# Keys in place, wider loads and write-backs on VectorE in a row-maximum kernel

## The chip, the cores and the metric

The kernel runs on one core of one Trainium2 chip. A core has several engines that run their own instruction streams and meet at semaphores; here ACT (ScalarE), POOL (GpSimd) and DVE (VectorE) compute, and SP (SyncE) issues the transfers, which 16 DMA engines carry out. TensorE is not used. The metric is the device time of one execution in microseconds, lower is better. The kernel before takes 1251.36 us, the median of 3 runs from 1251.27 to 1251.43.

## The reference

```python
x = np.random.randn(32, 2048, 2048).astype(np.float32)
x[np.random.rand(32, 2048, 2048) < 0.1] = np.nan

def reference(x, axis):          # axis = -1
    return np.nanmax(x, axis=axis).astype(np.float32)
```

The input is 65,536 rows of 2048 float32 values, 537 MB; about one value in ten is NaN. The output is the maximum of each row that leaves NaN out, 65,536 values. Each input byte is needed once.

## The kernel before, in words

**The arithmetic.** VectorE's maximum has to be kept from seeing a NaN. The kernel looks at the upper 16 bits of each float as a signed integer h. A finite value has h up to 0x7F7F, the NaN of this input has 0x7FC0. ACT computes a *key* from h with a Prelu (in `act`, called at line 493): for h up to 0x7F7F the key is 0x7F7F - h, for the NaN it is 0x7F7F + 128, as an unsigned 16-bit integer. A *write-back* then puts 0x7F7F - key into the upper half of the float. That gives h again for an ordinary value, and the upper half of minus infinity for a NaN. After that VectorE takes plain float maxima (a `tensor_reduce`, line 419 in `maxima`). Rows that were all NaN end as minus infinity and are turned into NaN at the end of each part of the output (`find`, lines 296 to 327).

**The tiles.** A tile holds some number of quarter rows for each of the 128 partitions; a quarter row is 512 floats. `TILES` (lines 17 to 46) is a plan written out by hand, one entry for each tile with three lists, all in quarter rows: the sizes of its loads; its chunks, each a pair of the sizes of the keys and the sizes of the write-backs; and the sizes of its maxima. A plain number among the write-backs is done by POOL; a pair `(n, w)` with w of 0 or more is done by ACT, w keys later; `(n, -1)` is done by VectorE, a case that the code has and the plan before does not use. So `([28], [([7], [7]), ([9], [9]), ([12], [12])], [16, 12])` is one load of 28 quarter rows (7 MB in all), three keys of 7, 9 and 12, three write-backs of the same sizes on POOL, and two maxima, of 16 and of 12. There are 74 tiles: one of 4, 46 of the kind just shown, and 27 others of 28 whose loads are cut ever finer towards the end; from tile 47 on ACT does some write-backs.

**Buffers.** Three input buffers `xt` of 28 quarter rows (`WIDE = 7` rows) take turns. Keys go to three separate dense 16-bit buffers `kt` of 12 quarter rows each (`KEYS`, `NKEYS`), so ACT reads every second half-word of `xt` and writes a dense `kt`; the write-back reads `kt` and writes every second half-word of `xt`. Before ACT reuses a `kt` it waits for the write-backs from it (`freed`, lines 379 to 389; `EARLY` names tiles that wait for the next buffer too).

**The order.** Each engine runs its instructions in the order in which the loop from line 440 issues them; `Order.add` puts a semaphore wait only where one is needed. For each tile the loads are issued first, then for each key: the key on ACT, the write-backs that it completes (`write`, lines 347 to 377), and every maximum whose quarter rows are all written back (`maxima`). The loads of tile n+3 (line 464, all on SP's queue) wait for the last maximum of tile n. `PARTS` gives after which tile a finished part of the output is fixed up on POOL, or on VectorE for the last one. The stores of the results come last on SP, after the last load.

Of the kernel before, what the change touches and what calls it, by code (L numbers as in the profile page):

```python
# [9 lines left out]
D = 2048  # L10

Q = D // 4
# [6 lines left out]
    + [([28], [([7], [7]), ([9], [9]), ([12], [12])], [16, 12])] * 46  # L19
# [6 lines left out]
    + [([28], [([7], [7]), ([9], [9]), ([12], [12])], [16, 12])] * 2  # L26
# [23 lines left out]
    tuple(range(1, 17)),  # L50
    tuple(range(17, 33)),
    tuple(range(33, 49)),
    tuple(range(49, 65)),
    (0,) + tuple(range(65, 74)),
# [5 lines left out]
    (0, 1, 16, 18),  # L60
    (1, 17, 32, 34),
    (2, 33, 48, 52),
    (3, 49, 64, 67),
    (4, 0, 72, None),
    (4, 73, 73, "dve"),
)

WIDE = 7
BUFS = 3

KEYS = 3 * D
NKEYS = 3
# [3 lines left out]
HEADS = 1  # L76
# [3 lines left out]
EARLY = tuple(range(47)) + (47, 48, 49, 50, 51, 52, 53, 54, 55, 56, 57, 58, 59, 60, 61, 68,)  # L80
# [105 lines left out]
def kernel(  # L186
# [15 lines left out]
    nc = tc.nc  # L202
# [15 lines left out]
    for tiles in GROUPS:  # L218
# [9 lines left out]
    firsts = [  # L228
        nc.alloc_sbuf_tensor(f"xt{i}", [P, WIDE * D], i32).ap() for i in range(HEADS)
    ]  # L230
    sing = ctx.enter_context(tc.tile_pool(name="sing", bufs=1))
    top, warm = scalars[:, 0:1], scalars[:, 1:2]
    xts = firsts + [
        sing.tile([P, WIDE * D], i32, name=f"xt{i}") for i in range(HEADS, BUFS)
    ]
    kts = [sing.tile([P, KEYS], u16, name=f"kt{i}") for i in range(NKEYS)]
# [23 lines left out]
    for number in range(HEADS):  # L260
        (c,) = TILES[number][0]
        gi, base = place[number]
        to = xts[number][:, 0 : c * Q]
        head = nc.sync.dma_start(  # L264
            out=dataclasses.replace(to, dep_tracking_offset=to.offset + P * WIDE * D),
            in_=groups[gi][0][:, base : base + c * Q],
        )
        tc.no_tile_sem_insts.add(head.ins.name)
        heads.append(head)

    with tc.tile_critical() as section:  # L271
# [75 lines left out]
        def write(number, a, b, k, kp, e, i, back):  # L347
            to = xts[number % BUFS][:, a:b].bitcast(i16)[:, 1::2]
            pair = pairs[number].get(i)
            name = pair and f"pair{number}_{pair[0]}"  # L350
            if back == "act":
                e = act(
                    [e], name, out=to, in_=kp, func=ACT.Copy, bias=float(TOP), scale=-1.0
                )
            else:
                kw = dict(
                    out=to,
                    in0=kp,
                    scalar1=-1.0,
                    scalar2=float(TOP),  # L360
                    op0=ALU.mult,
                    op1=ALU.add,
                )
                if back == "dve":
                    e = dve([e], nc.vector.tensor_scalar, **kw)
                else:
                    e = pool([e], name, **kw)
            state["clock"] += 1
            both = [(a, b, k, back, (state["clock"], order.count[back] + (back != "dve")))]
            if pair:  # L370
                if name not in half:
                    half[name] = both
                    return
                both += half.pop(name)
            for a, b, k, back, when in both:
                kfree[k][back] = max(kfree[k].get(back, ((0, 0), None)), (when, e))
                clean[number].append((a, b, e, back))
# [13 lines left out]
        def maxima(last):  # L391

            while state["tile"] <= last:
# [16 lines left out]
                xt = xts[number % BUFS]  # L410
# [29 lines left out]
        for number, (loads, chunks, reds) in enumerate(TILES):  # L440
# [3 lines left out]
            for ks, bs in chunks:  # L444
                assert sum(ks) * Q <= KEYS
# [12 lines left out]
            xt, before = xts[number % BUFS], free[number % BUFS]  # L458
            assert number < BUFS or state["tile"] > number - BUFS
            landed = []  # L460
# [21 lines left out]
            for step, c in enumerate(keys):  # L482
# [3 lines left out]
                if used + fresh.get(step, 0) > KEYS:  # L486
                    key = (key + 1) % NKEYS
                    used = 0
                    assert all(h[3] != key for h in held)
                    assert all(q[2] != key for v in half.values() for q in v)  # L490
                    kold = freed(key, (key + 1) % NKEYS) if number in EARLY and at + c == end else freed(key)
                    kfree[key] = {}
                e_key = act(
                    kold + here,
                    out=kts[key][:, used : used + c],
# [6 lines left out]
                used += c  # L502
# [104 lines left out]
```

## Time and profile before

| what | value |
|---|---|
| median of the runs | 1251.36 us |
| the profiled execution's own time | 1251.48 us |
| its span, first to last instruction | 1249.6 us |
| DVE busy | 1109.5 us (89%), 183 instructions |
| ACT busy | 980.1 us (78%), 286 |
| POOL busy | 1159.9 us (93%), 256 |
| data moved | 537.19 MB, mean 430 GB/s |
| the input queue's packets | 99.5% of the span of 16 DMA engines |

Busy is time in which an engine executes; the three engines work side by side, so the shares do not add. The rows of the profile name an engine, a line of the kernel, an operation, and what it writes and reads, output ahead of the arrow. All of ACT's work stands at line 277, POOL's write-backs at line 287 and VectorE's maxima at line 294, because helpers record them; `kt<-xt` on ACT is a key, `xt<-kt` a write-back, `acc<-xt` a maximum. Idle time is put down to what ended it.

### The profile page before, as it was taken

Reading aid. Unit: us, or ns where it says so; the run is one execution under the profiler, and the core shown is the slowest. Engines: PE = TensorE matmul, PEld = TensorE weight load, DVE = VectorE, ACT = ScalarE, POOL = GpSimd, SP = SyncE. Lnnn points to the kernel's source line nnn. Section 1 sums busy time; section 2 is a strip of 40 time slices with the busy share of each in tenths; the row PEclk is TensorE's granted clock in tenths of the full one; section 3 lists DMA queues with packets and bytes.
Section 4 is the critical chain, followed back from the end, with each engine's and each line's share of the span. In section 5 each row is a group of like instructions: output and inputs, shape, how many; then the busy total and the mean of one; then the engine's idle time right before and its main releaser. Section 6 shows DMA issues by size and latency. Waiting matters only on the chain.

```text
span 1249.6 us, 916 instructions
## 1 busy us (share of the span) xinstructions
DVE 1109.5 (89%) x183; ACT 980.1 (78%) x286; POOL 1159.9 (93%) x256
## 2 busy tenths in 40 slices
DVE  0888889888889888889888888988898999999999
ACT  3777777777777777777777777799877799999998
POOL 2999999999999999999999999967999987999988
DMA  9999999999999999999999999999999999999997
GB/s 415 441 411 441 441 441 430 423 441 441 437 415 441 441 439 426 428 441 439 437 419 439 441 439 430 424 441 439 437 422 436 439 437 433 422 436 428 429 429 316
DMA packets 16806, 537.19 MB, mean 430 GB/s; under 512 B 2592, under 2 KB 2592, under 8 KB 5152
## 3 DMA queue, kind: packets, MB, share of 16 engines
q1 hardware_dynamic: 16800, 537.14, 99.5%
q14 instruction: 6, 0.05, 0.0%
HBM read 536.87 MB, written 0.26 MB: 430 GB/s over the span
## 4 chain that ended last, share of the span: by engine, by line
POOL 37%; DVE 29%; DMA 25%; ACT 8%; issue 1%; SPq 0%
POOL xt L287 37%; DVE acc L294 29%; DMA xt<-in_x_dram 25%; ACT kt L277 7%; ACT xt L277 2%; POOL late L309 0%; POOL acc L323 0%; SPq L264 0%; SPq L469 0%; DVE acc L301 0%; SPq L602 0%; SPq L271 0%
## 5 line engine op out<-in xcount | busy, mean ns | idle before, releaser
L287 POOL TENSOR_SCALAR xt<-kt 128x3584 int16<-128x3584 uint16 (+10 forms) x241 | 1154.8, 4792 | 83.7 <-ACT kt L277 67.9
L294 DVE TENSOR_REDUCE acc<-xt 128x4 f32<-128x8192 f32 (+4 forms) x182 | 1109.3, 6149 | 137.8 <-POOL xt L287 130.9
L277 ACT ACTIVATE kt<-xt 128x3584 uint16<-128x3584 int16 (+10 forms) x252 | 913.9, 3663 | 262.5 <-DMA xt<-in_x_dram 222.6
L277 ACT ACTIVATE xt<-kt 128x512 int16<-128x512 uint16 (+7 forms) x32 | 68.6, 2145 | 0.7
L309 POOL TENSOR_SCALAR late<-acc 128x112 int32<-128x112 f32 (+1 forms) x5 | 2.8, 559 | 0.4
L323 POOL TENSOR_TENSOR acc<-acc,late 128x112 int32<-128x112 int32 (+1 forms) x5 | 2.0, 399 | 0.4
L277 ACT ACT_TABLE_LOAD x1 | 1.3, 1283 | 1.3 <-SPq L271 1.3
L329 POOL MEMSET scalars<- 128x1 f32 x1 | 0.1, 99 | 0.9 <-SPq L271 0.9
L588 POOL MEMSET const-float32-0.0<- 128x1 f32 x1 | 0.1, 99 | 0.2 <-issue 0.2
L277 ACT ACTIVATE scalars<-scalars 128x1 f32<-128x1 f32 x1 | 0.2, 203 | 0.0
L301 DVE SCALAR_TENSOR_TENSOR acc<-acc 128x7 f32<-128x7 f32 x1 | 0.2, 167 | 0.0
L588 POOL MEMSET const-bfloat16-1.0<- 128x1 bf16 x1 | 0.1, 102 | 0.0
L588 POOL MEMSET const-uint8-127<- 128x1 uint8 x1 | 0.1, 102 | 0.0
L588 POOL MEMSET const-float32-1.0<- 128x1 f32 x1 | 0.1, 99 | 0.0
## 6 DMA issues: line engine op xcount, KB each, us to landing
xt<-in_x_dram SPq DMA_DIRECT2D x62, 7168.0 KB, 22.5
xt<-in_x_dram SPq DMA_DIRECT2D x2, 4096.0 KB, 19.4
xt<-in_x_dram SPq DMA_DIRECT2D x2, 3584.0 KB, 25.6
xt<-in_x_dram SPq DMA_DIRECT2D x5, 1280.0 KB, 29.4
xt<-in_x_dram SPq DMA_DIRECT2D x4, 1536.0 KB, 24.2
xt<-in_x_dram SPq DMA_DIRECT2D x2, 3072.0 KB, 26.3
xt<-in_x_dram SPq DMA_DIRECT2D x1, 5632.0 KB, 19.5
xt<-in_x_dram SPq DMA_DIRECT2D x2, 2816.0 KB, 24.8
```

The costliest lines, as they stand in the source:

```text
L277: lambda: nc.scalar.activation(**kw),
L287: lambda: nc.gpsimd.tensor_scalar(**kw),
L294: return order.add("dve", nc.vector, lambda: do(**kw), deps)
L301: lambda: engine.scalar_tensor_tensor(out=acc, in0=acc, scalar=0.0, in1=acc, op0=ALU.mult, op1=ALU.add),
L309: lambda: engine.tensor_scalar(out=none, in0=acc, scalar1=LEAST, scalar2=float(0x00400000), op0=ALU.is_lt, op1=ALU.mult,),
L323: lambda: engine.tensor_tensor(out=bits, in0=bits, in1=none, op=ALU.add),
L329: e_top = order.add("pool", nc.gpsimd, lambda: nc.gpsimd.memset(top, EDGE), [])
L588: nc = _bacc.Bacc("TRN2", target_bir_lowering=False, num_devices=1)
```

## The change

- In tiles 0 to 37 (`PLAIN = 38`) the key is written over the upper half of its own float in `xt`, and the write-back reads it there. No `kt` is used and ACT has no wait for one.
- The three input buffers become parts of one tensor of 3 x 32 quarter rows. Tiles 0 to 35 (`FULL = 36`) use buffers of 32 quarter rows, later tiles buffers of 28 (`NARROW`); the space between these holds two of the three key buffers for the later tiles.
- 31 tiles have one load of 32 quarter rows; four more tiles of 32 have two loads. There are 69 tiles in place of 74.
- In tiles 1 to 37 and in a few later ones VectorE does one of the write-backs, 5 quarter rows in most, in the same form as POOL's (`tensor_scalar`).
- The sizes of the other tiles, the groups of rows, the parts of the output and the list `EARLY` follow from the new division.

```diff
-    + [([28], [([7], [7]), ([9], [9]), ([12], [12])], [16, 12])] * 46
...
+    + [([32], [([12], [(5, -1), 7]), ([12], [12]), ([8], [8])], [12, 12, 8])] * 31
+    + [([23, 9], [([18, 6], [(6, -1), 6, 12]), ([8], [8])], [12, 12, 8])]
+    + [([19, 13], [([12], [(5, -1), 7]), ([10], [10]), ([10], [3, 7])], [12, 12, 8])]
+    + [([12, 20], [([12], [(2, -1), 10]), ([12], [12]), ([8], [8])], [12, 12, 8])]
+    + [([15, 17], [([12, 8, 6, 6], [(2, -1), 10, 5, 7, 8])], [12, 12, 8])]
+    + [([28], [([9], [5, (4, -1)]), ([7], [7]), ([7], [7]), ([5], [5])], [4, 12, 12])]
+    + [([28], [([10], [(5, -1), 5]), ([6], [6]), ([9], [9]), ([3], [3])], [16, 12])]
...
+    + [([28], [([9], [9]), ([11], [11]), ([8], [(8, -1)])], [8, 20])]
...
+    + [([28], [([10], [10]), ([10], [10]), ([8], [(8, -1)])], [8, 20])]
...
-WIDE = 7
+WIDE = 8
+FULL = 36
+PLAIN = 38
+
+NARROW = (0, 17 * D // 2, 31 * D // 2)
...
+    full = nc.alloc_sbuf_tensor("xt", [P, BUFS * WIDE * D], i32).ap()
...
+    keys_ = full.bitcast(u16)
+    kts = [
+        sing.tile([P, KEYS], u16, name="kt"),
+        keys_[:, 14 * D : 14 * D + KEYS],
+        keys_[:, 45 * D : 45 * D + KEYS],
     ]
...
+    def room(number):
+        n = number % BUFS
+        if number < FULL:
+            return full[:, n * WIDE * D : (n + 1) * WIDE * D]
+        return full[:, NARROW[n] : NARROW[n] + 7 * D]
...
+            if number == PLAIN:
+                for k in (1, 2):
+                    kfree[k] = {"dve": ((0, 0), done_at[FULL - 1])}
...
-                if used + fresh.get(step, 0) > KEYS:
+                if number < PLAIN:
+                    key = 0
+                    kx = xt[:, at : at + c].bitcast(u16)[:, 1::2]
+                elif used + fresh.get(step, 0) > KEYS:
...
+                if number >= PLAIN:
+                    kx = kts[key][:, used : used + c]
+                    used += c
                 e_key = act(
                     kold + here,
-                    out=kts[key][:, used : used + c],
+                    out=kx,
                     in_=xt[:, at : at + c].bitcast(i16)[:, 1::2],
...
-                    kp = kts[key][:, used - (at - lo) : used - (at - lo) + n]
+                    kp = (
+                        kts[key][:, used - (at - lo) : used - (at - lo) + n]
+                        if number >= PLAIN
+                        else xt[:, lo : lo + n].bitcast(u16)[:, 1::2]
+                    )
```

More of the change, by code (lines that the diff above doesn't have):

```diff
@@ L78 @@
 LANES = 14
-EARLY = tuple(range(47)) + (47, 48, 49, 50, 51, 52, 53, 54, 55, 56, 57, 58, 59, 60, 61, 68,)
+EARLY = (0, 1, 2, 3, 4, 5, 6, 7, 8, 9, 10, 11, 12, 13, 14, 15, 16, 17, 18, 19, 20, 21, 22, 23, 24, 25, 26, 27, 28, 29, 30, 31, 32, 33, 34, 35, 36, 37, 38, 39, 40, 41, 42, 43, 44, 45, 46, 47, 48, 49, 50, 51, 52, 53, 54, 55, 56, 63)
 TOP = 0x7F7F
@@ L262 @@
         gi, base = place[number]
-        to = xts[number][:, 0 : c * Q]
+        to = room(number)[:, 0 : c * Q]
         head = nc.sync.dma_start(
-            out=dataclasses.replace(to, dep_tracking_offset=to.offset + P * WIDE * D),
+            out=dataclasses.replace(to, dep_tracking_offset=to.offset + P * BUFS * WIDE * D),
             in_=groups[gi][0][:, base : base + c * Q],
@@ L347, in write @@
         def write(number, a, b, k, kp, e, i, back):
-            to = xts[number % BUFS][:, a:b].bitcast(i16)[:, 1::2]
+            to = room(number)[:, a:b].bitcast(i16)[:, 1::2]
             pair = pairs[number].get(i)
@@ L375, in write @@
             for a, b, k, back, when in both:
-                kfree[k][back] = max(kfree[k].get(back, ((0, 0), None)), (when, e))
+                if number >= PLAIN:
+                    kfree[k][back] = max(kfree[k].get(back, ((0, 0), None)), (when, e))
                 clean[number].append((a, b, e, back))
@@ L409, in maxima @@
                 over.sort(key=lambda w: (w[3] == "act") == later)
-                xt = xts[number % BUFS]
+                xt = room(number)
                 lo = done - 1 if done % D else done
@@ L444 @@
             for ks, bs in chunks:
-                assert sum(ks) * Q <= KEYS
+                assert number < PLAIN or sum(ks) * Q <= KEYS
                 assert sum(ks) == sum(b[0] if isinstance(b, tuple) else b for b in bs)
@@ L457 @@
             xg = groups[gi][0]
-            xt, before = xts[number % BUFS], free[number % BUFS]
+            xt, before = room(number), free[number % BUFS]
             assert number < BUFS or state["tile"] > number - BUFS
+            if number == PLAIN:
+                for k in (1, 2):
+                    kfree[k] = {"dve": ((0, 0), done_at[FULL - 1])}
             landed = []
@@ L492 @@
                     kfree[key] = {}
+                if number >= PLAIN:
+                    kx = kts[key][:, used : used + c]
+                    used += c
                 e_key = act(
                     kold + here,
-                    out=kts[key][:, used : used + c],
+                    out=kx,
                     in_=xt[:, at : at + c].bitcast(i16)[:, 1::2],
```

31 lines of the change are left out of this document (12 added, 19 removed), and 44 rows, old and new, of the table TILES.

## The prediction

> Predicted: 1251.1 us, no change that a measurement can tell, because the 16 DMA engines already carry the input without a gap and the edit moves no byte less. What could spoil that is a new write-back on VectorE that has to fit into the period of one load.
>
> **What bounds the kernel now.** I read the busy shares by stage first, then the waits, then the chain that ended last, then the groups of one shape, then the end of the timeline. The five stages below are: first big load, one tile, tiles 2 to 61, the rest up to the store, and the end. Columns are length, busy time of each engine, clock, DMA share and GB/s.
>
> ```profile
> core 0: us, DVE busy (x) ACT busy (x) POOL busy (x), PEclk, DMA share, GB/s
> 0.00:22.49 22.49, 2.29 (x1) 3.40 (x3) 2.77 (x6) 1.00 0.98 414
> 22.49:39.43 16.94, 4.06 (x1) 12.45 (x4) 13.51 (x3) 1.00 1.00 433
> 39.43:1054.97 1015.54, 911.12 (x123) 779.72 (x191) 968.73 (x186) 1.00 1.00 434
> 1054.97:1242.53 187.56, 187.31 (x57) 182.40 (x87) 172.10 (x59) 1.00 1.00 427
> 1242.53:1249.60 7.07, 4.72 (x4) 2.12 (x3) 2.83 (x4) 1.00 0.14 37
> ```
>
> The DMA share is 1.00 from 22.49 to 1242.53 and the rate 434 GB/s in the long stage: transfers are never held up. The long stage is 60 loads of 28 quarter rows, 1015.54 / 60 = 16.93 us each, 0.6045 us a quarter row. POOL is busy 968.73 / 60 = 16.15 us of a period, VectorE 15.19, ACT 13.00. So POOL is near the period, but the transfers set it.
>
> ```profile
> ACT kt L277 <- DMA xt<-in_x_dram: 222.6, 63, 15.0
> DVE acc L294 <- POOL xt L287: 130.9, 59, 23.0
> ...
> ACT kt L277 <- POOL xt L287: 39.6, 59, 1.5
> ...
> SPq L469 <- DVE acc L294: 1151.7, 70, 37.8
> ```
>
> ACT waits for data, every engine behind it for the one ahead. SP's wait for VectorE is the ring of three buffers: the load of tile n+3 is issued after the last maximum of tile n. One turn of it, from the chain:
>
> ```profile
> 90.18 3.20 ACT kt L277
> 93.46 4.20 POOL xt L287
> 97.65 0.08 issue
> 97.73 5.35 POOL xt L287
> 103.11 15.16 DVE acc L294 x2
> 118.28 22.67 DMA xt<-in_x_dram
> ```
>
> The load is issued at 118.28 and lands 22.67 us later, though it takes 16.93: it stood behind the load ahead of it for 5.74 us. That is the room before the DMA engines could run dry. The end of the run:
>
> ```profile
> 0.74 0.37 SPq L264 DMA_DIRECT2D xt<-in_x_dram  x1
> ...
> 5.62 1.91 ACT L277 ACTIVATE kt<-xt 128x2048 uint16<-128x2048 int16 x1 [2.77 <-DMA xt<-in_x_dram]
> ...
> 1227.09 19.99 DVE L294 TENSOR_REDUCE acc<-xt 128x1 f32<-128x2048 f32 x9
> 1242.53 5.11 SPq L556 DMA_DIRECT2D out_dram<-acc  x3
> 1247.12 0.17 DVE L301 SCALAR_TENSOR_TENSOR acc<-acc 128x7 f32<-128x7 f32 x1
> ```
>
> The first store waits for the last load and leaves at 1242.53; VectorE ends at 1247.29, the span at 1249.6. The profiled execution took 1251.48 us, 1.88 outside its span, and stands 0.12 above the median of 1251.36.
>
> **The change part by part.** The prices, each the mean of its shape in ns, the figure ahead of a row's second bar:
>
> ```profile
> L294 DVE TENSOR_REDUCE acc<-xt 128x3 f32<-128x6144 f32 x61 | 399.2, 6545 | 1.1 <-POOL xt L287 1.1
> L287 POOL TENSOR_SCALAR xt<-kt 128x6144 int16<-128x6144 uint16 x51 | 359.2, 7042 | 4.5 <-ACT kt L277 0.6
> L277 ACT ACTIVATE kt<-xt 128x6144 uint16<-128x6144 int16 x60 | 319.3, 5322 | 35.7 <-POOL xt L287 35.5 <-DMA xt<-in_x_dram 0.2
> ...
> L287 POOL TENSOR_SCALAR xt<-kt 128x3584 int16<-128x3584 uint16 x57 | 239.2, 4197 | 23.9 <-ACT kt L277 20.5
> L277 ACT ACTIVATE kt<-xt 128x3584 uint16<-128x3584 int16 x59 | 188.1, 3189 | 199.0 <-DMA xt<-in_x_dram 198.2 <-POOL xt L287 0.7
> L294 DVE TENSOR_REDUCE acc<-xt 128x2 f32<-128x4096 f32 x27 | 118.4, 4412 | 0.2 <-POOL xt L287 0.2
> ...
> L287 POOL TENSOR_SCALAR xt<-kt 128x2560 int16<-128x2560 uint16 x8 | 24.4, 3055 | 2.0 <-ACT kt L277 1.6
> ...
> L277 ACT ACTIVATE xt<-kt 128x512 int16<-128x512 uint16 x10 | 7.7, 768 | 0.2
> ...
> L277 ACT ACTIVATE kt<-xt 128x512 uint16<-128x512 int16 x8 | 4.7, 613 | 0.0
> ...
> L277 ACT ACTIVATE xt<-kt 128x4096 int16<-128x4096 uint16 x1 | 4.8, 4767 | 0.0
> ```
>
> *Loads.* 31 loads of 32 quarter rows, 19.34 us each at the pace above, take the place of loads of 28; four more tiles of 32 come in two loads. Same bytes, 111 loads on SP before and after, no DMA added. Pieces of 64 KB a partition instead of 56 KB have no row: splitting or a slower long piece could cost, a longer piece could save. The pace is 434 GB/s with long pieces and 427 in the last stage with pieces down to 2 KB, so 8 KB more on an already long piece should be worth under 0.1%. I take 0, ends -1 and +2 us.
>
> *ACT.* In tiles 0 to 37 the key goes back into its own word, every second half-word, instead of into a dense buffer. A dense key costs (5322 - 3189) / 2560 = 0.833 ns an element. ACT's writes that land in every second half-word cost (4767 - 768) / 3584 = 1.116 ns, 0.197 us fixed. Nothing shows both sides strided over the same words. Ends: 0.833 (the reading alone was strided there already), and 1.40 if the same words on both sides cost that difference of 0.283 once more. I take 1.116, the row with the same output. Keys of 12, 12 and 8 quarter rows are then 7.05, 7.05 and 4.77, 18.9 us of 19.34. ACT would be the bound from (19.34 - 3 x 0.197) / 16384 = 1.144 ns. The waits for key buffers (39.6 us in all) go; ACT waits longer for data instead, so nothing is gained.
>
> *POOL.* It writes 27 of the 32 quarter rows, pieces of 7, 12 and 8: 4.20 + 7.04 + 4.77 (3584 and 512 more) + three issues of 0.08 = 16.25 us. It now also reads every second half-word; ACT read so at 0.833 ns. Ends: (7042 - 4197) / 2560 = 1.111 ns as before, and 1.39 with the same 0.283 added; taken 1.111. It binds from 1.335. Its four fix-ups for all-NaN rows go to other tiles; about 1.1 us each lies in POOL's idle 3 us.
>
> *VectorE.* Per tile it gains one write-back of 5 quarter rows, 2560 elements (W), and its maxima are 12, 12 and 8: 6.545 + 6.545 + 4.412, less two overlaps of 0.08 (15.16 in the chain for a pair whose means add to 15.23), 17.34. W has no row. VectorE's cheapest instruction, the 0.17 us one at 1247.12, is the low end; its rate of one element in (6545 - 4412) / 2048 = 1.042 ns with 0.145 fixed makes 2.81, and POOL's own 2560 takes 3.055, the high end. A maximum reads 4 bytes an element, W 2. By bytes W is a maximum of 1280 words, 1.48, which is also halfway between 0.17 and 2.81; I take 1.48. With 0.06 for the maximum's wait on W and 0.08 less where W follows, VectorE needs 18.8 us of 19.34 and fits up to W = 2.0.
>
> One tile, counted from its landing: keys end at 7.07, 14.12, 18.9. POOL writes 7 quarter rows from 7.14 to 11.34, 12 from 14.19 to 21.23, 8 to 26.1. In the first tile W follows POOL's 7; the maximum of 12 can start near 12.9, the second at 21.25 when POOL is done, and the third ends at 32.13. That is 12.8 us after the next landing (11.2 today: 118.28 less 90.18 and a period of 16.93), and the next W runs from 12.7 to 14.19. The load three on is issued 6.5 us before the engines run dry: no gap, and the pattern repeats. Behind SP's wait stand only later loads.
>
> *Tiles 36 to 68.* Tiles 36 and 37 need ACT 14336 x 1.116 + 4 x 0.197 = 16.8 of 16.93. The 8-quarter W of tiles 42 and 46 (0.145 + 4096 x 0.521 = 2.28) take VectorE to 17.3 against 16.93, 0.4 us of lag each; the room of over 5 us covers them and the next tiles, at 15.1, win back 1.8 each. The last eleven tiles, 308 quarter rows, have nearly the same maxima as before and cost VectorE about 167.5 us by these prices on either side.
>
> *The end.* The last landing stays near 1242.5. After it one quarter row still needs key 0.61, write-back 0.77, a whole-row maximum 2.28 (2048 x 1.042 + 0.145), the fix 0.17 and the store's 2.31 (1247.29 to 1249.6): 6.1, against 7.07 today. So the new end pieces can win at most 0.9; I take 0.3, between nothing and that.
>
> Sum: 1251.48 + 0 (loads) + 0 (ACT, POOL, VectorE, under the transfers) - 0.3 = 1251.2 as a profiled time; less 0.12, 1251.1.
>
> [...]
>
> **The rivals.**
>
> *VectorE and POOL shut each other out (slower).* For: W is due from 12.7 to 14.19 and POOL's long write at 14.19, and both work on the same words. Against: no wait in the trace shows maxima and POOL hindering each other, VectorE being busy 15.19 and POOL 16.15 of 16.93 us. If they exclude, the loop W + 7.04 + 0.02 + 10.88 - 0.08 = W + 17.86 has to stay under 19.34: it decides from W = 1.48, my own value. Above it the lag grows each tile; after 1.5 us W comes behind POOL's 12 and waits until 21.23. The tile then ends at 40.1, and three periods are 40.1 + 19.34 + 2.1 (issue to landing in an empty queue: 0.37 + 0.74 to 5.62, less 4 x 0.6045): 20.5 us each. Some 30 tiles x 1.15 = +34, 1285 us. [...]
>
> *VectorE becomes the bound (slower).* W at VectorE's known rate, 2.81: 20.1 against 19.34, 0.79 a tile. Room of 4.4 us (6.5 less 2.1) hides 6 tiles, 27 more pay: +21, 1272; at POOL's 3.055, 1279. For: one element in 1.042 ns is all that VectorE's rows show. Against: those read whole words.
>
> *Halves in place are dearer (slower).* ACT at 1.18 ns needs 19.9: 0.58 x 35 = +20, 1271; POOL at 1.39 needs 20.1, 1275. ACT at 1.40 would need 23.5, +147, 1398. For: no row reads and writes the same words strided. Against: reading strided costs ACT nothing above 0.833.
>
> *The end shortens and longer pieces speed the transfers (faster).* 0.9 and 1 us together, 1249.5; more has no row, so a gain over 0.2% (2.5 us, which is what I take a measurement of this kernel to tell from no change) is hardly to be had.
>
> **How the numbers follow.** Forecast 0.56 (own range 1249.9 to 1253.5, the load ends with the tail); shut out 0.15; VectorE the bound 0.12; halves dearer 0.10, of which the far end 0.02; a lag that the tiles of 28 don't win back, 2.5 to 6 us, 0.05; faster by more than 2.5 us 0.02. The range takes in the forecast, the lag, VectorE's bound and the near halves, 0.81: 1249.9 to 1279. Slower 0.15 + 0.12 + 0.10 + 0.05 = 0.42, same 0.56, faster 0.02.
>
> **What would show it.** Right: DMA share 1.00 and about 19.34 us between ACT's waits for data; ACT's in-place 6144 near 7.05 and POOL's at 7.04; VectorE's 2560 near 1.48 and starting about 12.7 us after a landing; the first store near 1242.5. Wrong: a gap in the DMA rate in the first three quarters; VectorE's 2560 at 2.8; waits of several us ahead of W with POOL busy, or POOL's writes drawn out beside W; ACT idle for data near zero.

## The result and the profile after

The changed kernel takes 1264.2 us (1261.87 to 1266.14, four runs), the kernel before 1251.39 beside it: a ratio of 1.0102 with a 95% interval of 1.0079 to 1.0125. It is slower by 12.8 us, where no change was forecast. The profiled execution took 1266.14 us, with a span of 1264.0.

The page of the changed kernel: the span, the busy times, and the rate in 40 slices of 31.6 us.

```profile
span 1264.0 us, 1010 instructions
DVE 1194.2 (94%) x251; ACT 1125.6 (89%) x275; POOL 1073.0 (85%) x248
GB/s 413 442 440 431 431 431 431 431 432 431 431 431 438 444 440 433 436 431 431 422 436 433 376 385 436 377 436 436 434 430 414 436 436 426 435 428 433 429 428 307
```

The first 22 slices stay around the full rate, a few per cent up and down. The worst slices, 376, 385 and 377, lie between 695 and 822 us. The busy time by stage, with columns as in the prediction: first wide load, one tile, tiles 2 to 31, the tiles in which the division changes, the rest up to the first store, and the end.

```profile
0.00:24.97 24.97, 2.29 (x1) 3.95 (x3) 2.76 (x6) 1.00 1.00 420
24.97:44.30 19.33, 8.21 (x2) 18.55 (x4) 11.06 (x2) 1.00 1.00 434
44.30:624.47 580.17, 567.60 (x121) 557.49 (x91) 487.13 (x95) 1.00 1.00 433
624.47:899.42 274.95, 268.65 (x47) 230.93 (x53) 232.23 (x48) 1.00 0.98 416
899.42:1256.92 357.50, 342.62 (x80) 312.54 (x124) 336.95 (x96) 1.00 1.00 426
1256.92:1263.95 7.03, 4.79 (x4) 2.12 (x3) 2.84 (x4) 1.00 0.15 37
```

30 wide tiles took 580.17 us, 19.34 each, as forecast. From 624 to 899 us the rate is 416 GB/s: (1 - 416 / 434) x 274.95 = 11.4 us. The first store leaves at 1256.92 instead of 1242.53, 14.4 later, and the stage behind it is as long as before. What engines waited for:

```profile
DVE acc L315 <- POOL xt L308: 44.4, 50, 10.7
...
SPq L494 <- DVE acc L315: 1165.8, 65, 43.6
```

VectorE's wait for POOL fell from 130.9 to 44.4, for VectorE now has little time left in a tile (567.60 of 580.17 us are busy in the stage of wide tiles). SP still waits for VectorE's last maximum. The groups that were priced:

```profile
L298 ACT ACTIVATE xt<-xt 128x6144 uint16<-128x6144 int16 x69 | 476.2, 6972 | 40.3 <-DMA xt<-in_x_dram 40.3
L308 POOL TENSOR_SCALAR xt<-xt 128x6144 int16<-128x6144 uint16 x34 | 246.0, 7236 | 80.2 <-ACT xt L298 80.0
L308 POOL TENSOR_SCALAR xt<-xt 128x3584 int16<-128x3584 uint16 x48 | 203.5, 4240 | 41.5 <-ACT xt L298 40.5
L315 DVE TENSOR_SCALAR xt<-xt 128x2560 int16<-128x2560 uint16 x33 | 60.8, 1843 | 19.0 <-ACT xt L298 19.0
```

The in-place forms cost what was forecast: ACT 6.97 (7.05 forecast), POOL 7.24 and 4.24 (7.04 and 4.20). W's mean, 1.84, is a mixture, as the timeline of a late wide tile shows:

```profile
598.61 1.62 DVE L315 TENSOR_SCALAR xt<-xt 128x2560 int16<-128x2560 uint16 x1
599.76 7.41 POOL L308 TENSOR_SCALAR xt<-xt 128x6144 int16<-128x6144 uint16 x1 [1.72 <-ACT xt L298]
```

W took 1.62. POOL's 12 quarter rows began 0.47 before W ended and took 7.41, 0.37 more than alone. Now the timeline behind the wide tiles: VectorE and POOL first, then SP's issues and ACT's starts on landing.

```profile
655.34 5.94 POOL L308 TENSOR_SCALAR xt<-xt 128x5120 int16<-128x5120 uint16 x1
657.04 5.67 DVE L315 TENSOR_SCALAR xt<-xt 128x2560 int16<-128x2560 uint16 x1
661.36 3.10 POOL L308 TENSOR_SCALAR xt<-xt 128x1536 int16<-128x1536 uint16 x1
...
771.22 6.43 DVE L315 TENSOR_SCALAR xt<-xt 128x2048 int16<-128x2048 uint16 x1
828.49 4.49 DVE L315 TENSOR_SCALAR xt<-kt 128x4096 int16<-128x4096 uint16 x1
...
680.19 0.33 SPq L494 DMA_DIRECT2D xt<-in_x_dram  x1
702.40 5.30 ACT L298 ACTIVATE xt<-xt 128x4608 uint16<-128x4608 int16 x1 [5.43 <-DMA xt<-in_x_dram]
718.38 0.33 SPq L494 DMA_DIRECT2D xt<-in_x_dram  x1
719.37 5.93 ACT L298 ACTIVATE xt<-xt 128x5120 uint16<-128x5120 int16 x1 [0.72 <-DMA xt<-in_x_dram]
736.51 0.33 SPq L494 DMA_DIRECT2D xt<-in_x_dram  x1
738.07 3.19 ACT L298 ACTIVATE xt<-xt 128x3584 uint16<-128x3584 int16 x1 [2.31 <-DMA xt<-in_x_dram]
756.22 0.33 SPq L494 DMA_DIRECT2D xt<-in_x_dram  x1
757.71 2.77 ACT L298 ACTIVATE xt<-xt 128x3072 uint16<-128x3072 int16 x1 [5.83 <-DMA xt<-in_x_dram]
777.61 3.19 ACT L298 ACTIVATE xt<-xt 128x3584 uint16<-128x3584 int16 x1 [7.56 <-DMA xt<-in_x_dram]
...
831.60 4.04 ACT L298 ACTIVATE xt<-xt 128x4608 uint16<-128x4608 int16 x1 [3.83 <-DMA xt<-in_x_dram]
```

A W of the same size took 5.67: POOL had begun 1.70 earlier, and W ended 1.43 after POOL did (661.28), while POOL's next 1536 elements, 1.91 where POOL ran alone (at 858.18), were drawn out to 3.10. The next two rows are later Ws that were held too: 2048 elements took 6.43, though 2560 take 1.62 when free, and 4096 took 4.49, where the prediction had 2.28. From 657 to 823 us VectorE is busy for 165.5 of 166 us, so it could not catch up. For the rest, call *lead* the time from a load's issue to the landing of the load ahead of it; it is what the prediction called the room. Before, it was 5.74. The load issued at 680.19, behind the held W and its three maxima, had a lead of 2.4, since the load ahead of it landed at 682.57 by the trace's landing record; it landed 19.8 us after that one. The load issued at 718.38 had a lead of 0.99 on the landing at 719.37 and landed 18.70 after it; the next two had 1.56 and 1.49 and landed 19.64 and 19.90 after the load ahead, where 16.93 is the pace. Seven loads of 28 quarter rows, from 702.40 to 831.60, took 129.2 us instead of 118.5: 10.7 of the 14.4 us. With the 2.9 of the load issued at 680.19 it is 13.6.

So three things could be the cause: VectorE held behind POOL, too much work for one engine there, or slots (input buffers) that come free too late for the transfers.

### The profile page after: what moved, and what is told of

The parts are those of the page before. It is cut to its first block, busy times and chain, and to the rows that moved or that the text cites. A ratio compares the mean times of both kernels' runs of the same rounds, so it can differ in the third digit from the quotient of the medians.

```text
span 1264.0 us, 1010 instructions
## 1 busy us (share of the span) xinstructions
DVE 1194.2 (94%) x251; ACT 1125.6 (89%) x275; POOL 1073.0 (85%) x248
## 4 chain that ended last, share of the span: by engine, by line
DVE 38%; DMA 30%; ACT 17%; POOL 14%; issue 1%; SPq 0%; DVEq 0%; ACTq 0%
DVE acc L315 36%; DMA xt<-in_x_dram 30%; ACT xt L298 16%; POOL xt L308 14%; DVE xt L315 2%; ACT kt L298 1%; POOL late L330 0%; POOL acc L344 0%; SPq L285 0%; DVE acc L322 0%; DVEq L182 0%; SPq L636 0%; ACTq L182 0%; SPq L292 0%
## 5 line engine op out<-in xcount | busy, mean ns | idle before, releaser
L315 DVE TENSOR_REDUCE acc<-xt 128x3 f32<-128x6144 f32 (+3 forms) x210 | 1113.4, 5349 | 48.6 <-POOL xt L308 44.4
L308 POOL TENSOR_SCALAR xt<-xt 128x3584 int16<-128x3584 uint16 (+11 forms) x198 | 922.1, 4657 | 180.2 <-ACT xt L298 171.8
L298 ACT ACTIVATE xt<-xt 128x6144 uint16<-128x6144 int16 (+10 forms) x214 | 948.2, 4526 | 117.8 <-DMA xt<-in_x_dram 117.1
L298 ACT ACTIVATE kt<-xt 128x6144 uint16<-128x6144 int16 (+11 forms) x43 | 142.0, 3322 | 13.9 <-POOL xt L308 11.8
L308 POOL TENSOR_SCALAR xt<-kt 128x2048 int16<-128x2048 uint16 (+9 forms) x35 | 143.7, 4107 | 4.8 <-ACT kt L298 2.8
L315 DVE TENSOR_SCALAR xt<-xt 128x2560 int16<-128x2560 uint16 (+3 forms) x38 | 75.9, 1997 | 19.0 <-ACT xt L298 19.0
L298 ACT ACTIVATE xt<-kt 128x1536 int16<-128x1536 uint16 (+4 forms) x16 | 36.9, 2309 | 0.4
L315 DVE TENSOR_SCALAR xt<-kt 128x4096 int16<-128x4096 uint16 x2 | 8.0, 4020 | 0.0
```

Of the source, the lines that this page charges most:

```text
L298: lambda: nc.scalar.activation(**kw),
L308: lambda: nc.gpsimd.tensor_scalar(**kw),
L315: return order.add("dve", nc.vector, lambda: do(**kw), deps)
```

## The experiments

All kernels are named by what they do; what was expected of each stands behind its edit, in the order of the text. In the expectations, *hold* means that VectorE's write-back is held by POOL's, *full port* (a name only: no run shows a port) that the two together have to fit into a period, *dense division* that the finer pieces give ACT and POOL too much, and *room theory* that a slot which comes free too late costs the time. The times in one table, the ratio with its 95% interval (a dash: a single run). The ratio is to the kernel before as measured beside each run, with medians from 1251.29 to 1252.45, so times in different lines compare to about 1 us.

| kernel | us | ratio |
|---|---|---|
| changed kernel | 1264.20 | 1.0102 [1.0079, 1.0125] |
| late W to POOL | 1264.68 | 1.0107 [1.0092, 1.0122] |
| the same, maxima of W's length on VectorE | 1265.38 | 1.0109 [1.0092, 1.0126] |
| W of 6 | 1304.31 | - |
| tiles 32 to 35 regular | 1259.23 | - |
| the same, without W in 36 to 46 | 1258.38 | 1.0058 [1.0043, 1.0073] |
| wide tiles, old division behind them | 1256.96 | 1.0040 [1.0026, 1.0054] |
| the same without W | 1256.37 | 1.0039 [1.0024, 1.0054] |
| before, keys in place | 1275.41 | 1.0192 [1.0177, 1.0207] |
| before, keys in place, halved loads | 1253.95 | 1.0015 [1.0005, 1.0024] |
| before, halved loads | 1253.81 | 1.0015 [1.0006, 1.0025] |
| before, maxima 8 and 20 | 1279.71 | 1.0228 [1.0212, 1.0243] |
| the same, halved loads | 1254.35 | 1.0021 [1.0012, 1.0031] |
| before, maxima 4 and 24 | 1302.51 | 1.0407 [1.0384, 1.0430] |
| old division, ACT helps POOL | 1257.57 | 1.0049 [1.0033, 1.0066] |
| old division, maxima 4, 12, 12 | 1255.95 | 1.0031 [1.0019, 1.0043] |
| old division, halved loads | 1268.79 | 1.0136 [1.0121, 1.0151] |
| the same, no W beside them | 1254.57 | 1.0021 [1.0011, 1.0031] |
| changed kernel, halved loads | 1287.81 | 1.0272 [1.0234, 1.0309] |

**First: is it the held W?** The nine Ws of tiles 32 to 46 go to POOL (four of them in the cut below); one kernel adds maxima of the same length on VectorE, so that only its sharing with POOL is gone and not its load.

```diff
-[(6, -1), 6, 12]   -[(5, -1), 7]   -[(2, -1), 10]   -(8, -1)
+[6, 6, 12]         +[5, 7]         +[2, 10]         +8
```

> Tiles 32 to 46 of the changed kernel with their nine VectorE write-backs given to POOL, in the same pieces; tiles 1 to 31 keep theirs. Theory (hold): in those tiles VectorE's write-back is held until the POOL instruction under way ends, VectorE falls behind, loads are issued late and the DMA engines run dry. Then the time is back at 1251 to 1253 us, the DMA share is 1.00 to the end and the first store leaves near 1242.5, although POOL has 2 to 3 us more to do in each of these tiles. Rival (dense division): ACT and POOL are simply overfull in tiles 32 to 37 through the finer pieces; then it stays at 1260 or more, since POOL gets still more work. Rival (VectorE's time): the write-backs cost only their own time on VectorE; then 1251 to 1253 too, and the filler run tells it apart.

> As the run before, and in the place of each of the nine write-backs VectorE runs a maximum over a small constant area, as long as an undisturbed write-back (0.27 us + 0.267 us a quarter row, 1.6 us for five), waiting for the same key; its result is not used. VectorE has the same added time at the same places, about 14 us in all, but nothing for which it could be held by POOL. Hold: 1251 to 1254. VectorE's time: 1260 to 1266, like the changed kernel. Dense division: 1260 or more.

1264.68 and 1265.38: nothing is won. POOL, which got the work, is now busy for 39.0 to 39.3 us of each 40 from 640 to 800 us, and the rate from 624 to 900 us is 418 GB/s against 415 in the changed kernel. So the held Ws alone don't set the time; with them gone POOL is full instead, and the time stays. VectorE's time alone and a division too fine for ACT and POOL are not told apart by these two runs.

**Second: does a longer W break the steady tiles?** W of 6 quarter rows instead of 5 in tiles 1 to 31.

```diff
-[(5, -1), 7]
+[(6, -1), 6]
```

> The changed kernel with one more quarter row given to VectorE in each of tiles 1 to 31: write-backs of 6 and 6 in place of 5 and 7. VectorE's own sum is 17.34 + 1.87 + 0.06 = 19.2 to 19.3 us of 19.34, POOL's falls by 0.6. Hold: the loop write-back, POOL's 12, two maxima is 1.87 + 17.86 = 19.7, over the period by 0.4; after some four tiles the write-back comes behind POOL's 12 and takes 6 to 8 us instead of 1.9, a load takes about 20.5 us, and the time is 1285 to 1300. Without any holding: 1262 to 1268, as the changed kernel.

The timeline of VectorE in this kernel, the last W that was short and the next one:

```profile
154.88 1.86 DVE L315 TENSOR_SCALAR xt<-xt 128x3072 int16<-128x3072 uint16 x1
174.40 8.66 DVE L315 TENSOR_SCALAR xt<-xt 128x3072 int16<-128x3072 uint16 x1
```

In seven tiles W takes 1.86 to 1.99 and comes a little later each time; in the eighth POOL's 12 quarter rows start first, and W takes 8.66. The kernel takes 1304.31 us (a single run), 40 more than the changed kernel and a little over the 1285 to 1300 expected. What the first rival of the prediction described is thus what these tiles show, W going from 1.99 us at the most to 8.66, and the changed kernel's W of 5 stays just short of it: its W starts 12.55 us after the landing in the second tile and 12.86 in the last of the 31.

**Third: which tiles cost what?** Tiles 32 to 35 as the 31 ahead of them (tiles 32 to 35 *regular*); the same without the Ws of tiles 36 to 46; 35 wide tiles with the division of before for the last 33 tiles (keys in place only up to tile 37); and that with POOL writing 12 quarter rows in place of W's 5 and its 7.

```diff
-31 tiles of 32, tiles 32 to 35 with divisions of their own
+35 tiles of 32, all [(5, -1), 7], [12], [8]
 second kernel, tiles 36, 37, 39, 42, 46:
-[5, (4, -1)]   -[(5, -1), 5]   -[8, (4, -1)]   -(8, -1)
+[9]            +[10]           +[8, (4, 0)]    +(8, 0)
 third: tiles 36 to 68 with the division of before
 fourth: [(5, -1), 7] -> [12] in the wide tiles
```

> Tiles 32 to 35 of the changed kernel divided like tiles 1 to 31: one load of 32, keys 12, 12, 8, a VectorE write-back of 5. Tiles 36 to 68 as they are. Hold: in tiles 32 to 35 the write-backs fall into POOL's gap and take 1.6 to 1.7 us; what those of tiles 36 to 46 lose stays, so 1255 to 1263. Dense division (of the four tiles with two loads): 1251 to 1254.

> The run with regular tiles 32 to 35 (1259.2), with the VectorE write-backs of tiles 36 to 46 taken away: in 36 and 37 POOL does its whole chunk, in 39, 42 and 46 ACT does the part (4, 8 and 8 quarter rows), which has 4 us to spare there. Full port: with neither a held write-back nor more work for POOL in 39, 42 and 46 most of the remaining 8 us go: 1251 to 1255. Rival (something else in the new division of tiles 36 to 46, such as keys in place in 36 and 37 or the order of the pieces): 1257 or more.

> 35 tiles like tiles 1 to 31 of the changed kernel (32 quarter rows in one load, keys in place, a VectorE write-back of 5), then the last 33 tiles as the kernel before divides them: no VectorE write-back there, ACT helps where it did before; only the first two of them keep their keys in place. What is known so far: giving the late write-backs to POOL, with or without a filler on VectorE, left the time at 1264 to 1265, and POOL was then busy throughout from 640 to 840 us. Theory (full port): VectorE's write-back and POOL's can't run at the same time, so the two together have to fit into a load's period beside the waits for ACT; the steady tiles fit, tiles 32 to 46 of the changed kernel do not, whoever does the writing. Then wide loads, in-place keys and the write-back of 5 cost nothing by themselves: 1251 to 1253, DMA share 1.00. Rival (the wide tiles leave VectorE or POOL behind, which the tiles of 28 can't win back): 1256 or more.

> As the run before, with the write-back of 5 on VectorE given to POOL: one POOL write-back of 12 in its place, no VectorE write-back anywhere. POOL then needs 7.04 + 7.04 + 4.77 + 0.24 = 19.1 of 19.34 us a tile. Full port: 1251 to 1253, so that the write-back on VectorE was not needed for the wide tiles; DVE idles 2 us a tile on POOL. Rival (POOL falls behind, 19.1 being too near the period): 1255 or more with POOL busy without a break.

Regular tiles 32 to 35 take off 5 us (a single run), and their Ws take 1.67 to 1.70, not 5.67. The late Ws cost nothing that shows (1259.23 to 1258.38), and the old division behind tile 36 takes off another 1.4, within the intervals. What is left, 5.6 us, is there without any new division and with or without W; the 1251 to 1253 that I had expected of both kernels was wrong. In the third kernel the step from 32 to 28 quarter rows looks so, SP's issues and ACT's starts on landing:

```profile
682.59 7.01 ACT L289 ACTIVATE xt<-xt 128x6144 uint16<-128x6144 int16 x1 [0.83 <-DMA xt<-in_x_dram]
715.69 0.33 SPq L485 DMA_DIRECT2D xt<-in_x_dram  x1
717.36 4.18 ACT L289 ACTIVATE xt<-xt 128x3584 uint16<-128x3584 int16 x1 [0.25 <-DMA xt<-in_x_dram]
734.48 0.33 SPq L485 DMA_DIRECT2D xt<-in_x_dram  x1
735.02 3.19 ACT L289 ACTIVATE xt<-xt 128x3584 uint16<-128x3584 int16 x1 [1.42 <-DMA xt<-in_x_dram]
753.73 3.19 ACT L289 ACTIVATE xt<-xt 128x3584 uint16<-128x3584 int16 x1 [0.96 <-DMA xt<-in_x_dram]
```

The slot of the tile that landed at 682.59 is loaded again 33.1 us later. In the wide stage the two loads behind it would take 38.7 us, a lead of 5.6; here they are loads of 28, and the lead is 1.67, then 0.54. The load behind the second landed 18.71 after the one ahead. Tiles of 28 quarter rows behind wide ones leave less time to cover what the wide ones need from landing to reload.

The landing records of the profiled executions tell how much of the loss this is. Add up how much later than the pace of 0.6045 us a quarter row each load landed between 640 and 905 us: 13.8 us in the changed kernel, 7.7 with regular tiles 32 to 35, 5.7 with the old division, 4.8 without W, 0.0 in the kernel before. The last load of all landed 14.4, 7.7, 5.9 and 5.3 us later than before. So nearly all of the loss lies in a handful of loads around the step.

**Fourth: is the lead what counts?** Four kernels without any wide tile or W. In the kernel before, tiles 1 to 44 with keys in place; with maxima of 8 and 20, and of 4 and 24, instead of 16 and 12, which leaves the work of each engine as it was and only moves the end of the last maximum; and the one with keys in place again, with loads of twice 14, so that the first key starts when half a tile is there.

```diff
-PLAIN: all keys in dense buffers
+PLAIN = 45: keys of tiles 0 to 44 in place
 other kernels, tiles 1 to 46:
-[16, 12]
+[8, 20]   or   [4, 24]
 last kernel, tiles 1 to 44, keys in place:
-[28]
+[14, 14]
```

> The kernel before with its division unchanged and one part of the change alone: in tiles 0 to 44 the keys stay in place. ACT's keys cost 1.11 ns an element instead of 0.83, 16.2 to 16.5 us of 16.93 a tile; its waits for key buffers go. Full port: no change, 1251 to 1252. Rival (in-place keys make the chain from landing to maximum too long): 1254 or more.

> As the run with 4 and 24, with maxima of 8 and 20: a slot comes free about 19.95 + 10.8 = 30.8 us after its landing, 1 us inside the 31.8 of the room theory: 1251 to 1252.5. If time grows with the length of the last maximum without a limit in between, about half of what the cut of 4 and 24 costs: 1257 to 1262.

> The kernel before, keys dense as there, with the maxima of the 46 tiles cut 4 and 24 instead of 16 and 12: the same work for every engine, nothing in place. The last maximum can start when GpSimd ends, 19.95 us after the landing, and takes some 12.95 for 24 quarter rows, so a slot comes free about 32.9 us after its landing where 28.1 did before. Room theory: 32.9 is over 31.8, so the loop of load, keys, last maximum and load again sets the pace at some 17.3 us a tile instead of 16.93: 1263 to 1272, with less than 430 GB/s from the first tiles on and loads that find an empty queue. Without such a limit (only the busiest engine and the transfers count): 1251 to 1252.

> The kernel before with keys in place in tiles 0 to 44 (the earlier run of that took 1275.4, +24), and here the loads of tiles 1 to 44 come as two of 14 quarter rows. The first keys then start when half a tile has landed, so ScalarE and GpSimd run ahead of the landing, and the time from landing to last maximum, 31.3 us in the earlier run, falls by a few us, while no key gets cheaper. Room theory (a ring slot must be free about 31.8 us after its landing, two loads of 16.93 less 2.1 from issue to landing): nearly all of the +24 goes; 44 further loads cost some 3 us at most: 1251.5 to 1257, and 430 GB/s or more in the first 700 us. Rival, that the halves in place are dearer in themselves (ScalarE or GpSimd, at 16.2 to 16.8 us a tile, set the pace): 1273 to 1278, and 404 to 432 GB/s as in the earlier run.

The stage from 60 to 740 us, one line each: before, keys in place, maxima 8 and 20, maxima 4 and 24, keys in place with halved loads.

```profile
60.00:740.00 680.00, 608.41 (x82) 500.81 (x121) 667.93 (x125) 1.00 1.00 434
```

```profile
60.00:740.00 680.00, 591.25 (x79) 631.04 (x118) 645.94 (x122) 1.00 0.99 420
```

```profile
60.00:740.00 680.00, 588.98 (x78) 482.10 (x116) 644.45 (x121) 1.00 0.99 419
```

```profile
60.00:740.00 680.00, 574.78 (x76) 469.49 (x114) 628.47 (x118) 1.00 0.98 409
```

```profile
60.00:740.00 680.00, 607.05 (x82) 650.14 (x121) 663.55 (x125) 1.00 1.00 433
```

No engine is full in any of them: POOL, the busiest, has 12 to 52 us of 680 left. With the same work the maxima of 8 and 20 cost 27 us and those of 4 and 24 50 us. Keys in place cost 24 us with whole loads and nothing with halved ones, next to the control below, although ACT and POOL do the same work in both. The cost is therefore not in the keys but in when the slot comes free. Two loads of 16.93 less the time from landing to next issue give the lead that would be there at full pace: before 33.86 - 28.1 = 5.8; keys in place 33.86 - 31.3 (39.34 to 70.62) = 2.6; maxima 8 and 20, in the lines below, 33.86 - 30.9 (337.44 to 368.31) = 3.0.

```profile
337.44 3.19 ACT L277 ACTIVATE kt<-xt 128x3584 uint16<-128x3584 int16 x1 [4.10 <-DMA xt<-in_x_dram]
351.40 0.33 SPq L469 DMA_DIRECT2D xt<-in_x_dram  x1
355.07 3.19 ACT L277 ACTIVATE kt<-xt 128x3584 uint16<-128x3584 int16 x1 [4.81 <-DMA xt<-in_x_dram]
368.31 0.33 SPq L469 DMA_DIRECT2D xt<-in_x_dram  x1
373.96 3.19 ACT L277 ACTIVATE kt<-xt 128x3584 uint16<-128x3584 int16 x1 [6.06 <-DMA xt<-in_x_dram]
```

The load issued at 351.40 had a lead of 3.67 and still landed 18.89 us after the load ahead. My expectation had put the limit at 2.1 us, the time from issue to landing in an empty queue, and so had expected no loss with 8 and 20 and a third of the loss measured with 4 and 24; that was wrong, in the size of the limit. The kernel before, where its lead was smallest in this stage:

```profile
339.68 0.33 SPq L469 DMA_DIRECT2D xt<-in_x_dram  x1
...
344.22 3.19 ACT L277 ACTIVATE kt<-xt 128x3584 uint16<-128x3584 int16 x1 [3.00 <-DMA xt<-in_x_dram]
361.11 3.19 ACT L277 ACTIVATE kt<-xt 128x3584 uint16<-128x3584 int16 x1 [3.06 <-DMA xt<-in_x_dram]
```

4.54 us of lead, and the next landing 16.89 later: enough. The limit is not sharp. By the landing records of the kernel with maxima of 8 and 20, loads with a lead of 3.0 to 3.5 us landed 1.6 us late in the mean (8 loads), with 3.5 to 4.0 it was 0.8 (10), with 4.0 to 4.3 0.5 (9), and with 4.3 to 4.6 0.1 (9).

**Fifth: the controls.** Halved loads alone, and halved loads with the maxima of 8 and 20.

```diff
 tiles 1 to 44:
-[28]
+[14, 14]
 second kernel also:
-[16, 12]
+[8, 20]
```

> The kernel before with the loads of tiles 1 to 44 as two of 14: what smaller loads cost by themselves. The kernel before has the room already, so nothing can be won but the start of the last tiles: 1251 to 1254, and what it is above 1251.4 is to be taken off the 1253.95 of the run with keys in place and halved loads. If smaller loads are faster in themselves, 1249 or less, the gains of the halved loads in other runs say nothing on room.

> The kernel with maxima of 8 and 20 (1279.7), its loads of tiles 1 to 44 as two of 14. Room theory: the keys and writes start earlier after the landing of the whole tile, the last maximum ends some 3 to 5 us earlier, and the 28 us go: 1251.5 to 1256. If the order of the maxima costs by itself (VectorE waits for GpSimd in each tile): 1275 to 1281.

Halved loads by themselves cost 1.9 us (0.0015 x 1251.5), and the kernel with keys in place has the same ratio: nothing is left for the keys. The 27 us of the maxima of 8 and 20 go as well, to 1254.35. The same cut of the same work costs 27 us or some 0.8 (1.0021 less 1.0015), by how early the first key may start.

**Sixth: at the step itself.** Three kernels on the one with the old division: ACT takes 6 of POOL's quarter rows in tiles 38 to 41; the maxima of tiles 36 to 41 are cut 4, 12, 12, so that the first one waits for POOL's first write alone; the loads of tiles 25 to 43 are halved. Two more kernels follow: the changed kernel with halved loads in tiles 21 to 31 and 36 to 46, and the third one without W in tiles 25 to 35.

```diff
-([12], [12])         -[16, 12]      -[32]       -[28]
+([12], [(6, 0), 6])  +[4, 12, 12]   +[16, 16]   +[14, 14]
 last kernel, on the third, tiles 25 to 35:
-[(5, -1), 7]
+12
```

> The 35 wide tiles followed by the division of before (1256.96, 5.6 above before), with 6 of GpSimd's 28 quarter rows of writing back given to ScalarE in each of tiles 38 to 41. GpSimd then has some 3.4 us a tile to spare there, where it had 0.1, and ScalarE 16.2 becomes some 18 to 19 less the denser keys. Backlog theory (GpSimd leaves the wide tiles late and cannot win it back at 16.83 of 16.93 us a tile): the stretch of 404 to 413 GB/s at 680 to 800 us shrinks, 1252.5 to 1255. If the loss lies in the loads of those tiles, or ScalarE becomes late in GpSimd's stead: 1256 to 1259.

> The 35 wide tiles with the division of before behind them (1256.96), the maxima of tiles 36 to 41 cut 4, 12, 12 instead of 16, 12: 0.2 us a tile more for VectorE, but its first maximum waits for GpSimd's first write alone, so the last one ends some 1.4 us earlier after the landing (VectorE waited 1.65 us a tile for GpSimd's second write there). Room theory: the loads are issued 1.4 us earlier, leads of 0.5 to 2.6 us become 2 to 4: 1252.5 to 1255.5. If GpSimd's 16.8 us a tile set the pace behind the step: 1256 to 1258.

> The 35 wide tiles with the division of before behind them (1256.96), with the loads of tiles 25 to 35 as two of 16 quarter rows and of tiles 36 to 43 as two of 14: no work of any engine is changed or moved, the first key alone can start half a load earlier, so ScalarE gains 0.7 us a tile on the landing, up to its whole lead, and GpSimd enters the tiles of 28 quarter rows earlier. Room theory: nearly all of the 5.6 us goes, 1251.5 to 1254, and no 40 us from 680 to 800 under 425 GB/s. If the loss is work that GpSimd has too much of: 1256 to 1258.

> The changed kernel (1264.2) with the loads of tiles 21 to 31 as two of 16 and of tiles 36 to 46 as two of 14; nothing else. Room theory: ScalarE and GpSimd enter the tiles 33 to 46 with up to 6 us of lead, the landings do not wait for slots, 1252 to 1257, though writes of VectorE may still be held 2 to 6 us behind GpSimd. If the held writes and GpSimd's work set the time by themselves, whatever the lead: 1262 to 1266.

> The run with smaller loads in tiles 25 to 43 (1268.8), in which in tiles 25 to 35 GpSimd writes 12 quarter rows in one instruction in place of VectorE's 5 and its own 7. If the 12 us came from VectorE's writes, which in that run took 5.25 to 7.70 instead of 1.6 because GpSimd had no idle time of 1.9 us in front of them any more: 1255 to 1259, as without smaller loads (1256.4 to 1257), since GpSimd then has 19.0 of 19.33 us a tile to do and gains nothing on the landing. If smaller loads themselves do harm in the wide tiles: 1265 to 1270.

Help for POOL did not pay: 1257.57, no better. The rate rose from 410 to 424 GB/s at 760 to 800 us, but the dip ahead of that, 413 from 680 to 760, stayed. POOL's work in tiles 38 to 41 is therefore not what sets the loss; the help starts only with tile 38, which lands near 735 us, so a backlog of POOL ahead of that is not ruled out. Maxima of 4, 12, 12 gave 1255.95, 1 us in the direction expected but within the intervals. Halved loads made things worse, 1268.79 and, on the changed kernel, 1287.81, against my expectation. The timeline of the first of these shows why:

```profile
520.65 7.05 POOL L300 TENSOR_SCALAR xt<-xt 128x6144 int16<-128x6144 uint16 x1 [0.98 <-ACT xt L290]
521.44 7.70 DVE L307 TENSOR_SCALAR xt<-xt 128x2560 int16<-128x2560 uint16 x1
527.78 5.95 POOL L300 TENSOR_SCALAR xt<-xt 128x4096 int16<-128x4096 uint16 x1
```

ACT, no longer bound to whole landings, ran ahead, so POOL's 12 quarter rows began 0.79 us before W was due. In the wide tiles W had always found POOL waiting for a key (1.2 to 2.7 us of idle time in the changed kernel, "<-ACT" in POOL's rows); that gap was gone, W took 7.70, and POOL's next 4096 elements 5.95 instead of 4.77. From 500 to 624 us the rate was 402 GB/s. In the changed kernel with halved loads it is the same, the first held W taking 8.52. With W given to POOL and all else the same it was 434 there:

```profile
500.00:624.00 124.00, 112.16 (x20) 123.78 (x21) 122.33 (x22) 1.00 1.01 434
```

That kernel takes 1254.57, 14 us less than with W, and 1.8 less than the kernel without W and with whole loads (ratios 1.0021 and 1.0039, whose intervals just overlap). Its rate from 624 to 900 us is 432 GB/s, and its loads land 2.3 us late between 640 and 905 us, against 4.8 with whole loads. With W gone, earlier first keys seem to help at the step too. No kernel here beat the one before: its transfers already run at 434 GB/s in its long stage, and no stage of the tables here runs faster, so I see little to win.

## Why the prediction was wrong

- *Loads.* Right: 19.34 us a load of 32, at 433 to 434 GB/s. Fewer, longer pieces brought nothing and cost nothing.
- *ACT.* Right: 7.05 forecast, 6.97 measured for 6144 elements; the wait for key buffers fell from 39.6 to 11.8 us.
- *POOL.* The rate was right; a write that starts beside W takes up to 0.4 us longer in the steady tiles (7.42 at the most for 6144 elements, against 7.04), and 1.5 in the first one (5.71 for 3584 elements, against 4.20), which was not in the sum.
- *VectorE.* W was forecast at 1.48 and took 1.58 to 1.70 wherever POOL did not hold it. A quarter row more took 0.28 us more, by the shortest of each: 1.86 for a W of 6, 1.58 for one of 5. The tile came out as counted: W due 12.7 after the landing, measured 12.55 to 12.86; a lead of 6.5 us for the next load but two, measured 6.4 (issue at 579.38, landing ahead of it at 585.81).
- *The rival that VectorE and POOL shut each other out.* The rows show W held (8.66 with W of 6, 7.70 with halved loads, 5.67 in the changed kernel, where W ends 1.4 us after the instruction of POOL's that was under way) and POOL drawn out beside W (3.10 for 1536 elements, 1.91 where it ran alone). What the two engines share no run shows. The place was wrong. The prediction's loop decides from W = 1.48, but with W at 1.58 to 1.70 its start moves by only 0.31 us over 30 tiles: POOL waits for a key when W is due, and with W = 1.62 it lost 0.37 us where its write began 0.47 before W ended. W of 6, at 1.86 to 1.99, was over the point and cost 40 us more than W of 5, so the point lies between.
- ***Tiles 36 to 68* is the step that failed.** It said of 0.4 us of lag that "the room of over 5 us covers them". It counted the room of a steady stage. At the step from wide tiles to tiles of 28 the room is 1.67, then 0.54 us, even with regular wide tiles and no late W, since the wide tile's time from landing to reload meets two shorter loads. The Ws of 8 were priced at 2.28 and took 4.49 and 3.56; those of tiles 36, 37 and 39, which had no price, took 3.13, 4.53 and 6.43; and nothing was won back, VectorE being busy throughout. The divisions of tiles 32 to 35 were not worked out at all; W took 5.67 us there. By the medians, 5.6 us are the step (1251.4 to 1257.0), 5.0 tiles 32 to 35 (1264.2 to 1259.2, a single run), and 2.2 the late Ws and the division behind tile 36, which the intervals do not tell from nothing.
- *The size of the room.* The prediction took 2.1 us as what a load must be ahead. The cut of 8 and 20, with 3.0 us at full pace, lost 27 us: it needs more, some 4.3 in that run, where loads landed 0.5 us late in the mean with a lead of 4.0 to 4.3 and 0.1 with 4.3 to 4.6.
- *The end.* The stage behind the first store is 7.03 us (7.07 before): as good as nothing won, 0.3 forecast.
- *The chances.* "A lag that the tiles of 28 don't win back, 2.5 to 6 us, 0.05" was the nearest case in kind; it came to 12.8.

Not settled: why tiles 32 to 35 cost the same with their Ws on POOL. POOL is then full there, which fits, but no run gave both engines less. Nor is the cause of the late slots at the step itself shown by a repair: help for POOL, earlier maxima and halved loads without W took off about 2 us at most, the last two in the direction expected.

## What to carry to other kernels

In a ring of buffers, write down for each tile the time from landing to the end of its last reader, and set it against the loads that follow *that* tile: a change of tile size, or of the order in which the last reader runs, can cost more than any engine's busy time shows: here 27 us by the cut of the maxima alone, with some 35 us of 680 left to the busiest engine. The price of an instruction can be a property of the schedule: W of 5 took 1.58 to 1.70 us where POOL was idle when it was due, and 4.53 and 5.67 in the changed kernel, 7.70 and 8.52 with halved loads, where a write of POOL's had begun ahead of it. A repair that lets one engine run ahead can take such a gap away, as the halved loads did (1256.96 to 1268.79).

## What the runs showed of the hardware

- Loads that are issued late showed in the rate and hardly in the DMA share: from 60 to 740 us 409 GB/s at a share of 0.98 with maxima of 4 and 24, 419 at 0.99 with 8 and 20, against 434 at 1.00 before. By the packet records of the traces a packet of 57,344 bytes took 2.12 us at the median in these two kernels and in the changed one, as before, but one in a hundred took over 3.0 us in the two and over 2.98 in the changed kernel, where it is 2.12 before.
- In the kernel with maxima of 8 and 20 the loads that were issued less than some 4.3 us ahead of the landing in front of them landed late in the mean (by 0.5 us at 4.0 to 4.3, by 1.6 at 3.0 to 3.5), though the first load of the kernel before, with nothing ahead of it, landed 2.1 us after its issue less its own time. Behind a load that was itself late, less did: 2.5 us in the changed kernel, from 699.87 to 702.40, with the next landing 16.97 later. The sixteen landing records of one load of 28 quarter rows lie 0.32 to 1.32 us apart, first to last, in the kernel before; in the changed kernel it is 3.20 in the load that landed at 702.40, 0.70 and 0.62 in the next two, and 2.34 to 3.02 in all behind those. What this spread does to the next load was not tried by a run of its own.
- The time for which W was held stood inside its own duration, not in a wait: the wait lists of the changed kernel have one row for W, of 19.0 us on ACT ahead of the first tile's, and none on POOL. Only its rows and the means of the groups show it: 1.84 for 2560 elements beside 1.62 in the steady tiles, and 4.78 for 2048.
